# GpSimd's instructions chained in program order, with a job's transfers spaced eight chunks apart

## The chip, the cores and the metric

The kernel runs on one core of a Trainium2 chip. The metric is the device time of one execution in microseconds. Before the change three runs took 2229.27, 2233.75 and 2235.53 us, so the median is 2233.75. The profile was taken of a further execution of 2231.67 us.

## The reference

A trunk of two pre-norm residual layers over 256 tokens of width 2048, all in float32. Layer 0 mixes tokens with two-dimensional neighbourhood attention (16 heads of 128, a 4 x 64 grid, a window of 16 columns), layer 1 with a gated short convolution. After each mixer comes a gated MLP of inner width 5632 with a centred convolution of width 3 before the gate. A final RMSNorm closes it.

```python
def conv_glu_ffn(x, w_up, conv_w, conv_b, w_down):
    h = dwconv_centered(x @ w_up, conv_w) + conv_b
    g, u = jnp.split(h, 2, axis=-1)
    return (jax.nn.silu(g) * u) @ w_down

for i in range(DEPTH):                      # i = 0: attention, i = 1: short conv
    a = rms_norm(h, mix_norm[i])
    h = h + mixer(a)
    h = h + conv_glu_ffn(rms_norm(h, ffn_norm[i]), ...)
return rms_norm(h, final_norm)
```

The work is in the weight matrices: q, k, v and output of the attention, input and output of the convolution mixer, and two pairs of up- and down-projections.

## The kernel before

**Precision.** Every float32 operand is split into a high and a low part in the fast matmul format: ScalarE casts the high part (L186 for weights, L294 for activations), VectorE subtracts to get the low part (L189, L295). A product of two tiles is then three matmuls (high x high, high x low, low x high). In the projections with feature rows on the partitions (`Phase`: q and k, both up-projections, the convolution's input) the two parts of the activation lie side by side, so the first pass is one matmul of 512 columns (L255) and the second, with the low weights, one of 256 (L263).

**Chunks and items.** All weights arrive as chunks of up to 512 KB, in one list. `prep_to` goes along that list: it loads a chunk on SP's queue into one of six `raw` buffers and splits it. Matmul work is a list of items. The main loop takes them in order; for each it prepares its chunks, issues its matmuls, then prepares some chunks ahead (six after an up-projection item, four elsewhere) and calls `tick`, which runs delayed work that has come due. An up-projection item has two feature tiles, 64 matmuls and four chunks; there are 22 in a half of the MLP, or 27 with a few single ones at its start.

**Units with seven products.** In the output projections (`Tokens`) two blocks of 128 inner rows and two halves of the columns make a 2 x 2 block product. Written plainly, a pair costs eight products; the plans at L53 to L58 mark some pairs with H, and these take seven (`seven`, L460), with sums of blocks as operands. A plan holds the order of the pairs, the set of H, and the delay in ticks of `combine` (L486), which adds the unit's four extra accumulators into the residual stream. A unit needs two things made beforehand:

- sums of activations (`make_forms`, L513): four subtractions and additions on GpSimd (L519 to L522) into a tile `s`, as soon as the second of two neighbouring activation tiles is there. Four ticks later (`LATE`) ScalarE and VectorE split them (`splits`, into tiles `sf` and others). This happens during the up-projection, for the down-projection behind it; in an MLP half at every second item where the pair is marked.
- sums of weights, a *job* (`make`, L194): three transfers copy blocks of the weights to a piece of DRAM (`kept`), then two transfers on GpSimd's queue add another block to the first and second copy (L204, L205), then a third adds the first sum to the third copy (L208). The unit later loads the sums from there in place of weights (`kept` chunks in `prep_to`).

**Where jobs lie.** A job is an entry in the chunk list that loads nothing. `Phase` spreads its jobs over the items `hosts[0]` to `hosts[1]`, `Values` puts one after every second pair of chunks. The jobs' adding transfers are delayed by a number of chunks from the job: `ADDS, STORES = 2, 5` (L75). A group of jobs runs one phase or more ahead of the units that use it.

**Who orders the instructions.** Each engine runs its instructions in one fixed order, and a framework's scheduler sets that order from the program order and from what is ready. `load` (L160) forces weight loads on SP's queue into program order. The job's copies go through `load` too: each is queued behind the last weight load, but doesn't become the one that later loads are queued behind (`strict=False`). GpSimd's instructions have no such rule: the four form operations, the additions of mask and bias (L600), and the adding transfers stand as the scheduler puts them. A transfer issued by GpSimd waits on GpSimd for what it reads and writes, and what stands behind it waits too.

**The end.** The last down-projection keeps the last two pairs for `finale` (L445), which finishes one block of the output after the other, while the final norm of the blocks already done is computed.

Of the kernel before, what the change touches and what calls it, by code (L numbers as in the profile page):

```python
# [18 lines left out]
ALU = mybir.AluOpType  # L19
# [6 lines left out]
KT = D // P  # L26
NH = 16
GRID_W = 64
# [17 lines left out]
def plan(text, due):  # L46


    words = text.split()
    return (tuple(int(x[1:]) for x in words), {int(x[1:]) for x in words if x[0] == "H"}, due)  # L50


S_FIRST = (plan("P0 H1 H3 P2 H4 H5 P8 H6 H7 H9 P10", 3), plan("P0 P2 H1 H3 P8 H4 H5 H6 P10 H7 H9", 6))  # L53
S_SECOND = plan("P0 P2 H1 H3 H4 P9 H5 H6 H7 H8 P10", 0)
S_MLP = {(0, 0): S_FIRST, (0, 1): (S_SECOND, plan("P0 P2 P5 H1 H3 H4 P9 H6 H7 H8 P10", 0)),
         (1, 0): S_FIRST, (1, 1): (plan("P0 P2 H1 H3 H4 P9 H6 H7 H8 P5 P10", 1), plan("P0 P2 H1 H3 P5 H4 H6 H7 P8 P9 P10", 0))}
S_OUT = (plan("P0 H1 H2 P3 H4 H5 P6 P7", 1), plan("P0 P3 H1 H2 P6 H4 H5 P7", 0))
S_ATT = (plan("P0 P1 P2 H6 P3 H7 P4 P5", 1),) * 2  # L58
QK_JOBS, V_JOBS, UP_JOBS, SC_JOBS = (0, 2, 2, 0), (2, 2, 2, 0), (11, 10, 8, 10), 15


HEAD = (2, 4)
# [9 lines left out]
C_END = C_ID + P  # L72

LEAD = 96
ADDS, STORES = 2, 5  # L75
LATE = 4
RAWS = 6

# [2 lines left out]
def trunk(ctx, tc, xT, par, bias, wqk, wv, wo, wsc, wscout, wup, wdown, out):  # L81
    nc = tc.nc
# [44 lines left out]
    prepped = []  # L127

    stores = []
# [30 lines left out]
    def load(out, in_, strict=True):  # L160

        with ExitStack() as order:
            if "SP" in newest:
                order.enter_context(tc.issue_after(newest["SP"].ins))
            last = nc.sync.dma_start(out=out, in_=in_)
        if strict:
            newest["SP"] = last
# [24 lines left out]
    kept, newest, fenced = {}, {}, []  # L192

    def make(w, g, i):  # L194

        kept[id(w), g, i] = dst = dp.tile([P, 3, 4 * P], F32, name=f"kept{len(kept)}")
        l, r, t = (w[8 * g + f:8 * g + f + 4, :, (2 * i + k) * P:(2 * i + k + 1) * P].rearrange("f p c -> p f c")
                   for f, k in ((0, 0), (4, 0), (4, 1)))
        at = [dst[:, n].rearrange("p (f c) -> p f c", f=4) for n in range(3)]
        for n, x in ((0, l), (1, t), (2, t)):  # L200
            load(at[n], x, False)

        def adds():
            nc.gpsimd.dma_start(out=at[0], in_=r, accum_op=ALU.add)  # L204
            nc.gpsimd.dma_start(out=at[1], in_=r, accum_op=ALU.add)  # L205

        def store():
            nc.gpsimd.dma_start(out=at[2], in_=at[0], accum_op=ALU.add)  # L208
        stores.append((len(prepped) + ADDS, adds))
        stores.append((len(prepped) + STORES, store))  # L210

    jobs = []

    def plan_jobs(w, plans):
        jobs.extend((w, g, i) for g, (order, sset, _) in enumerate(plans) for i in order if i in sset)

    def take(n):
        out, jobs[:] = jobs[:n], jobs[n:]
        return out
# [54 lines left out]
    def after(n, fn):  # L274
        later.append((at[0] + n, fn))

    item = [0]
    at = [0]
# [9 lines left out]
    def split_into(hi, lo, src):  # L288

        with ExitStack() as order:  # L290
            if fenced:
                for x in ("ACT", "DVE"):
                    order.enter_context(tc.issue_after(newest[x].ins))
            first = nc.scalar.copy(out=hi, in_=src)  # L294
            nc.vector.tensor_sub(out=lo, in0=src, in1=hi.bitcast(F32))  # L295
        return first

    def split(dst, src):
        return split_into(dst[:, :S], dst[:, S:], src)
# [202 lines left out]
    def form_slots(blocks):  # L502

        if not form_at:
            return [left_over.pop() for _ in range(3)]
        tag = next(x for x in form_at if blocks == 3 or x != "sf")
        form_at.remove(tag)
        y = tp.tile([P, (6 if tag == "sf" else 8) * P], F32R, name="sf", tag=tag)
        if tag != "sf" and blocks == 3:
            left_over.append(y[:, 6 * P:])  # L510
        return y

    def make_forms(xe, xo, place, fresh=False):  # L513

        if fresh:
            form_at[:], left_over[:] = ("sf", "vv", "qk") * 2, ()
        v = tp.tile([P, 4, P], F32, name="s", tag="s")
        x11, x21, x12, x22 = (x[:, t * P:(t + 1) * P] for x in (xe, xo) for t in range(2))
        nc.gpsimd.tensor_sub(out=v[:, 0, :], in0=x21, in1=x22)  # L519
        nc.gpsimd.tensor_sub(out=v[:, 1, :], in0=v[:, 0, :], in1=x11)  # L520
        nc.gpsimd.tensor_add(out=v[:, 3, :], in0=x12, in1=v[:, 1, :])
        nc.gpsimd.tensor_sub(out=v[:, 2, :], in0=x11, in1=x21)  # L522
# [51 lines left out]
    a2 = [None] * KT  # L574
# [6 lines left out]
    def qk_evac(f, ps):  # L581
        c = both(ps, "g" if waiting and len(held) % 2 else "corr")
        if waiting:
            held.append(lambda: qk_rest(f, c))
        else:
            qk_rest(f, c)

    def qk_rest(f, c):
        h, which = divmod(f, 2)
        x = heads[h]  # L590
        t = tp.tile([P, S], F32, name="qk", tag="conv", bufs=4)
        nc.vector.tensor_mul(out=t, in0=c, in1=rstd)
        if which == 0:
            x["qk"] = tp.tile([P, 4 * S], F32R, name="qk", tag="qk")
        x["qk"[which]] = x["qk"][:, which * 2 * S:(which + 1) * 2 * S]
        first = split(x["qk"[which]], t)
        if which == 0:
            b = tp.tile([P, 6 * GRID_W], F32, name="bias", tag="sf")
            nc.sync.dma_start(out=b, in_=bias[:, h, :])
            nc.gpsimd.tensor_add(out=b.rearrange("p (i c) -> p i c", c=GRID_W),  # L600
                                 in0=b.rearrange("p (i c) -> p i c", c=GRID_W),
                                 in1=mask.unsqueeze(1).broadcast_to([P, 6, GRID_W]))
            x["b"] = b
        else:
            after((FIRST_HEADS[h] if h < len(FIRST_HEADS) else HEAD)[0], lambda: scores(h))
        return first
# [234 lines left out]
    def mlp(layer, a, evac):  # L841
        for half in range(2):
            act, forms = [None] * HALF, {}
            lo = half * HALF
            Phase(wup[layer], [f for j in range(lo, lo + HALF) for f in (2 * j, 2 * j + 1)], KT, a,
                  up_evac(layer, act, forms, S_MLP[layer, half]), intro=0 if half else 3,
                  jobs=take(UP_JOBS[2 * layer + half]), hosts=(3, 16) if half else (8, 22))
            Tokens(down[layer, half], HALF, act, evac if half else residual, S_MLP[layer, half], forms,
                   halves=4 if half and layer else 0)

# [2 lines left out]
    for half in range(2):  # L853
        plan_jobs(down[0, half], S_MLP[0, half])
    plan_jobs(wscout, S_OUT)
    for half in range(2):
        plan_jobs(down[1, half], S_MLP[1, half])
    for g in range(NH // 4):
        Phase(wqk, range(8 * g, 8 * g + 8), KT, a0, qk_evac, intro=0 if g else INTRO, step=STEP,
              jobs=take(QK_JOBS[g]), hosts=(0, 4))  # L860
        Values(g, a0, take(V_JOBS[g]))
    Tokens(wo, KT, oT, to_norm(1, a1), S_ATT, oforms)
    mlp(0, a1, to_norm(2, a2))
    Phase(wsc, range(3 * KT), KT, a2, sc_evac, intro=3, jobs=take(SC_JOBS), hosts=(8, 29))
    Tokens(wscout, KT, yT, to_norm(3, a3), S_OUT, yforms)
    mlp(1, a3, last_evac())


# [47 lines left out]
    for item[0], (ph, ft, c, k0, ka, kb) in enumerate(items):  # L916

        with ExitStack() as order:
# [4 lines left out]
            if item[0] != KT // STEP * INTRO:  # L923
# [3 lines left out]
                end, n = ends[item[0]], FURTHER if getattr(ph, "fence", False) else AHEAD  # L927
# [77 lines left out]
```

## Time and profile before

| | |
|---|---|
| runs, median (lowest to highest) | 2233.75 us (2229.27 to 2235.53) |
| profiled execution | 2231.67 us, span 2229.9 us |
| granted TensorE clock, mean | 0.992 |
| busy: PE, VectorE, ScalarE, GpSimd | 98%, 78%, 58%, 14% |
| jobs and units with seven products | 64 |

On the page each instruction group stands with its source line, so L189 is the low-part split of weights and L263 the low-part pass of a projection. PE busy is the time with a matmul under way. `kept<-in_wdown` is a job's copy if SP issued it, and an adding transfer if GpSimd (POOL) did; `kept<-kept` is the third adding transfer. A wait is put down to what came last. The chain of waits goes back from an instruction to what released it.

### The profile page before, as it was taken

To read this page: it belongs to the slowest core of one execution; us is meant where nothing else is said; L and a number is where in the kernel's file an instruction comes from. 1 tells how busy PE (TensorE), PEld (TensorE's weight loads), DVE (VectorE), ACT (ScalarE), POOL (GpSimd) and SP (SyncE) were. 2 spreads that over 40 slices of the span, in tenths; PEclk is the share of its full clock that TensorE was granted. 3 is DMA by queue.
4 is the path that set the end of the run, shared out by engine and by line. 5 is a ranking of instruction groups with operands and counts; after the bars stand their busy time and mean duration, and the time that the engine had idled before them with its cause. 6 is when DMAs were issued, how large, how long until landed. Compare 5 with 4: busy or idle time off the path is not lost.

```text
span 2229.9 us, 33099 instructions
## 1 busy us (share of the span) xinstructions
PE 2193.6 (98%) x11716; PEld 1900.0 (85%) x11716; DVE 1737.6 (78%) x2650; ACT 1286.3 (58%) x1985; POOL 308.2 (14%) x347
## 2 busy tenths in 40 slices
PE   9999999999899999999999999999999999999998
PEld 8788888888788888888888888888888888888886
DVE  8677667876688877788995676888768898778887
ACT  7555556654566655566664454666656666556565
POOL 1222010122200022200002222002220001221000
PEclk9999999999999999999999999999999999999999
DMA  9999557899868899967789999869996788998685
GB/s 285 273 280 253 183 167 229 239 270 250 233 212 269 264 278 256 267 206 228 251 269 279 270 297 268 282 221 266 278 226 203 243 274 278 262 279 236 200 263 170
DMA packets 411222, 555.32 MB, mean 249 GB/s; under 512 B 21680, under 2 KB 314672, under 8 KB 411056
## 3 DMA queue, kind: packets, MB, share of 16 engines
q1 hardware_dynamic: 332880, 502.23, 68.6%
q0 software_dynamic: 76800, 50.34, 17.1%
q8 instruction: 92, 1.51, 0.3%
q10 hardware_dynamic: 1376, 0.63, 0.1%
q14 instruction: 74, 0.61, 0.1%
HBM read 551.03 MB, written 102.76 MB: 293 GB/s over the span
## 4 chain that ended last, share of the span: by engine, by line
PE 79%; DMA 10%; DVE 5%; ACT 3%; issue 2%; POOL 1%; SPq 0%; DVEq 0%; ACTq 0%; POOLq 0%
PE mm L255 30%; PE mm L263 16%; DMA kept<-in_wdown 9%; PE mm L456 6%; PE mm L458 6%; PE mm L457 6%; PE mu L456 3%; PE mu L458 3%; PE mu L457 3%; DVE lo L189 2%; ACT hi L186 1%; PE mm L686 1%; PE mm L688 1%; PE mm L687 1%; PE tr L364 1%
## 5 line engine op out<-in xcount | busy, mean ns | idle before, releaser
L189 DVE TENSOR_TENSOR lo<-raw,hi 128x1024 fp32r<-128x1024 f32 (+1 forms) x856 | 1016.3, 1212 | 133.4 <-ACT hi L186 66.9
L186 ACT CAST hi<-raw 128x1024 fp32r<-128x1024 f32 (+1 forms) x920 | 914.5, 1010 | 347.1 <-PE mm L458 120.0
L255 PE MATMUL mm<-a,hi 128*128 128x512 f32 x4096 | 966.0, 392 | 0.4 <-DVE a L303 0.3
L255 PEld LDWEIGHTS mm<-a,hi 128*128 128x128 f32 x4096 | 762.9, 189 | 154.2 <-DVE a L303 1.2
L263 PEld LDWEIGHTS mm<-a,lo 128*128 128x128 f32 x4096 | 518.9, 193 | 34.9 <-DVE lo L189 22.5
L263 PE MATMUL mm<-a,lo 128*128 128x256 f32 x4096 | 526.7, 285 | 20.9 <-DVE lo L189 20.9
L332 ACT ACTIVATE conv<-pad,pt 128x256 f32<-128x256 f32 x176 | 105.6, 601 | 269.1 <-DVE pad L324 268.9
L456 PE MATMUL mm<-hi,act 128*128 128x512 f32 x634 | 247.5, 390 | 0.4 <-DVE corr L319 0.3
L458 PE MATMUL mm<-hi,act 128*128 128x512 f32 x634 | 246.7, 389 | 0.0
L457 PE MATMUL mm<-lo,act 128*128 128x512 f32 x576 | 224.4, 390 | 0.0
L334 DVE SCALAR_TENSOR_TENSOR conv<-pad,pt,conv 128x256 f32<-128x256 f32 x384 | 185.1, 484 | 34.9 <-ACT conv L332 25.9
L204 POOL DMA_DIRECT2D kept<-in_wdown x52 | 67.5, 1297 | 672.3 <-DMA kept<-in_wdown 671.9
L456 PEld LDWEIGHTS mm<-hi,act 128*128 128x128 f32 x634 | 119.0, 188 | 25.5 <-DVE corr L319 1.3
L458 PEld LDWEIGHTS mm<-hi,act 128*128 128x128 f32 x634 | 119.0, 188 | 24.8
L457 PEld LDWEIGHTS mm<-lo,act 128*128 128x128 f32 x576 | 108.2, 188 | 21.8
L319 DVE TENSOR_TENSOR corr<-mm,corr 128x256 f32<-128x256 f32 x256 | 106.2, 416 | 20.2 <-ACT corr L318 20.2
L318 ACT COPY corr<-mm 128x256 f32<-128x256 f32 x256 | 85.9, 368 | 60.2 <-PE mm L263 59.8
L208 POOL DMA_DIRECT2D kept<-kept x64 | 54.8, 855 | 400.9 <-DMA kept<-in_wdown 292.5
L295 DVE TENSOR_TENSOR sf<-s,sf 128x384 fp32r<-128x384 f32 (+2 forms) x37 | 19.1, 522 | 114.0 <-ACT sf L294 113.9
L295 DVE TENSOR_TENSOR act<-conv,act 128x256 fp32r<-128x256 f32 x88 | 37.6, 428 | 88.6 <-ACT act L294 88.6
L205 POOL DMA_DIRECT2D kept<-in_wdown x52 | 82.2, 1580 | 8.0 <-DMA kept<-in_wdown 7.0
L294 ACT CAST sf<-s 128x384 fp32r<-128x384 f32 (+2 forms) x37 | 17.2, 466 | 111.6 <-POOL s L520 102.7
(164 smaller groups left out, 1752.4 us busy)
## 6 DMA issues: line engine op xcount, KB each, us to landing
raw<-in_wup SPq DMA_DIRECT2D x352, 512.0 KB, 5.9
raw<-in_wdown SPq DMA_DIRECT2D x124, 512.0 KB, 4.8
raw<-in_wsc SPq DMA_DIRECT2D x96, 512.0 KB, 7.2
kept<-in_wdown SPq DMA_DIRECT2D x156, 256.0 KB, 8.6
raw<-kept SPq DMA_DIRECT2D x64, 512.0 KB, 5.0
raw<-in_wqk SPq DMA_DIRECT2D x56, 512.0 KB, 5.9
kept<-in_wdown POOLq DMA_DIRECT2D x104, 256.0 KB, 10.0
raw<-in_wv SPq DMA_DIRECT2D x32, 512.0 KB, 5.4
```

The costliest lines, as they stand in the source:

```text
L186: newest["ACT"] = nc.scalar.copy(out=hv, in_=r)
L189: newest["DVE"] = nc.vector.tensor_sub(out=lv, in0=r, in1=hv.bitcast(F32))
L205: nc.gpsimd.dma_start(out=at[1], in_=r, accum_op=ALU.add)
L255: nc.tensor.matmul(self.ps[ft], lhsT=prepped[i][0][:, o:o + P], rhs=self.src[k], start=k == 0, stop=False)
L263: nc.tensor.matmul(self.ps[ft][:, S:], lhsT=prepped[i][1][:, o:o + P], rhs=self.src[k][:, :S], start=False, stop=k == self.nk - 1)
L318: nc.scalar.copy(out=corr, in_=ps[:, S:])
L319: nc.vector.tensor_add(out=corr, in0=ps[:, :S], in1=corr)
L332: nc.scalar.activation(c, x[:, 1:S + 1], AF.Identity, scale=w[1], bias=b)
L334: nc.vector.scalar_tensor_tensor(out=c, in0=x[:, tap:tap + S], scalar=w[tap], in1=c, op0=ALU.mult, op1=ALU.add)
L456: nc.tensor.matmul(ps, lhsT=xh, rhs=wh, start=start, stop=False)
L457: nc.tensor.matmul(ps, lhsT=xh, rhs=wl, start=False, stop=False)
L458: nc.tensor.matmul(ps, lhsT=xl, rhs=wh, start=False, stop=stop)
```

## The change

Three things change together.

1. A new helper `pool` queues each instruction that it is given behind the previous one that it was given, on GpSimd: the four form operations, the bias addition, the adding transfers. GpSimd's order is then the program's.
2. The three copies of a job are issued by GpSimd, through the same helper, in place of SP. The first two adding transfers come eight chunks behind the job (`ADDS = 8`) in place of two, the third sixteen chunks behind it in place of five.
3. There are 67 units in place of 64: one more in the second half of layer 0's MLP and two more in that of layer 1's, where the plans of the two column groups are rewritten. The jobs are dealt out anew, and the items that host them begin earlier and end later: items 1 to 20 in place of 3 to 16 in second halves, 4 to 25 in place of 8 to 22 in first halves, 4 to 27 in place of 8 to 29 in the convolution's input.

```diff
-S_MLP = {(0, 0): S_FIRST, (0, 1): (S_SECOND, plan("P0 P2 P5 H1 H3 H4 P9 H6 H7 H8 P10", 0)),
-         (1, 0): S_FIRST, (1, 1): (plan("P0 P2 H1 H3 H4 P9 H6 H7 H8 P5 P10", 1), plan("P0 P2 H1 H3 P5 H4 H6 H7 P8 P9 P10", 0))}
+S_MLP = {(0, 0): S_FIRST, (0, 1): (S_SECOND, S_SECOND),
+         (1, 0): S_FIRST, (1, 1): (plan("P0 P2 H1 H3 H4 P9 H5 H6 H7 H8 P10", 0), plan("P0 P2 H1 H3 H4 P5 H6 H7 H8 P9 P10", 0))}
...
-QK_JOBS, V_JOBS, UP_JOBS, SC_JOBS = (0, 2, 2, 0), (2, 2, 2, 0), (11, 10, 8, 10), 15
+QK_JOBS, V_JOBS, UP_JOBS, SC_JOBS = (0, 2, 2, 0), (2, 2, 2, 0), (11, 11, 10, 11), 14
...
-ADDS, STORES = 2, 5
+ADDS = 8
...
         for n, x in ((0, l), (1, t), (2, t)):
-            load(at[n], x, False)
-
-        def adds():
-            nc.gpsimd.dma_start(out=at[0], in_=r, accum_op=ALU.add)
-            nc.gpsimd.dma_start(out=at[1], in_=r, accum_op=ALU.add)
-
-        def store():
-            nc.gpsimd.dma_start(out=at[2], in_=at[0], accum_op=ALU.add)
-        stores.append((len(prepped) + ADDS, adds))
-        stores.append((len(prepped) + STORES, store))
+            pool(nc.gpsimd.dma_start, out=at[n], in_=x)
+
+        def first():
+            for n in range(2):
+                pool(nc.gpsimd.dma_start, out=at[n], in_=r, accum_op=ALU.add)
+
+        def second():
+            pool(nc.gpsimd.dma_start, out=at[2], in_=at[0], accum_op=ALU.add)
+        stores.append((len(prepped) + ADDS, first))
+        stores.append((len(prepped) + 2 * ADDS, second))
+
+    def pool(op, **of):
+
+        with ExitStack() as order:
+            if "POOL" in newest:
+                order.enter_context(tc.issue_after(newest["POOL"].ins))
+            newest["POOL"] = op(**of)
...
-        nc.gpsimd.tensor_sub(out=v[:, 0, :], in0=x21, in1=x22)
...
+        pool(nc.gpsimd.tensor_sub, out=v[:, 0, :], in0=x21, in1=x22)
...
-            nc.gpsimd.tensor_add(out=b.rearrange("p (i c) -> p i c", c=GRID_W),
+            pool(nc.gpsimd.tensor_add, out=b.rearrange("p (i c) -> p i c", c=GRID_W),
...
-                  jobs=take(UP_JOBS[2 * layer + half]), hosts=(3, 16) if half else (8, 22))
+                  jobs=take(UP_JOBS[2 * layer + half]), hosts=(1, 20) if half else (4, 25))
...
-    Phase(wsc, range(3 * KT), KT, a2, sc_evac, intro=3, jobs=take(SC_JOBS), hosts=(8, 29))
+    Phase(wsc, range(3 * KT), KT, a2, sc_evac, intro=3, jobs=take(SC_JOBS), hosts=(4, 27))
```

The other three form operations are wrapped in the same way.

More of the change, by code (lines that the diff above doesn't have):

```diff
@@ L518, in make_forms @@
         x11, x21, x12, x22 = (x[:, t * P:(t + 1) * P] for x in (xe, xo) for t in range(2))
-        nc.gpsimd.tensor_sub(out=v[:, 0, :], in0=x21, in1=x22)
-        nc.gpsimd.tensor_sub(out=v[:, 1, :], in0=v[:, 0, :], in1=x11)
-        nc.gpsimd.tensor_add(out=v[:, 3, :], in0=x12, in1=v[:, 1, :])
-        nc.gpsimd.tensor_sub(out=v[:, 2, :], in0=x11, in1=x21)
+        pool(nc.gpsimd.tensor_sub, out=v[:, 0, :], in0=x21, in1=x22)
+        pool(nc.gpsimd.tensor_sub, out=v[:, 1, :], in0=v[:, 0, :], in1=x11)
+        pool(nc.gpsimd.tensor_add, out=v[:, 3, :], in0=x12, in1=v[:, 1, :])
+        pool(nc.gpsimd.tensor_sub, out=v[:, 2, :], in0=x11, in1=x21)
         if isinstance(place, tuple):
```

## The prediction

> **What bounds the kernel now.** I read the head of the page first, then the waits by engine.
>
> ```profile
> span 2229.9 us, 33099 instructions
> PE 2193.6 (98%) x11716; PEld 1900.0 (85%) x11716; DVE 1737.6 (78%) x2650; ACT 1286.3 (58%) x1985; POOL 308.2 (14%) x347
> POOL kept L204 <- DMA kept<-in_wdown: 671.9, 38, 143.1
> POOL kept L208 <- DMA kept<-in_wdown: 292.5, 48, 8.7
> ACT sf L294 <- POOL s L520: 102.7, 24, 11.2
> SPq L165 <- DVE lo L189: 1324.8, 699, 16.5
> PE mm L263 <- DVE lo L189: 20.9, 8, 5.2
> PE tr L639 <- DVE act L295: 4.5, 1, 4.5
> ```
>
> (Columns of the waits: total us, times, longest.) The matmul engine is busy 98% of the span, so a change pays by removing matmuls or by removing the few waits of PE. One group of waits is large: eight times the second half of an up-projection item (the low-part matmuls of L263) waits for VectorE's split L189, 20.9 us together. VectorE is not full (78%), so I followed the chain of waits back from the longest of the eight.
>
> ```profile
> 578.42 8.68 DMA kept<-in_wdown
> 587.38 0.87 POOL kept L208
> 589.29 0.52 ACT sf L294
> 589.84 0.35 DVE sf L295
> 590.60 1.14 DVE lo L189
> 591.79 3.79 PE mm L263 x16
> ```
>
> GpSimd issued a first adding transfer at 578.42, then stood 8.68 us until it had landed, because the second one (L208) is next in its order. The form of the activations (L519 to L522) sat behind that wait. ScalarE's and VectorE's splits of the form stood in their own orders, and the weight splits that PE needed stood behind them. GpSimd's and SP's timelines just before show a whole job, and what the copies have to do with it:
>
> ```profile
> 564.24 1.28 POOL L204 DMA_DIRECT2D kept<-in_wdown  x1 [2.33 <-DMA kept<-in_wdown]
> 578.42 1.28 POOL L204 DMA_DIRECT2D kept<-in_wdown  x1 [2.87 <-DMA kept<-in_wdown]
> 563.90 4.73 SPq L165 DMA_DIRECT2D raw<-in_wup  x4
> 568.69 3.21 SPq L165 DMA_DIRECT2D kept<-in_wdown  x3
> ```
>
> The copies (three per job, last row) stand in SP's order behind weight loads that wait for free buffers (1324.8 us in all), and GpSimd waits for them at L204 (2.33 and 2.87 us here), and then for its own first transfer at L208.
>
> **What the eight waits cost.** A clean item lasts 11.11 us (491.53 to 502.64). PE's timeline gives the four disturbed stretches, each from the start of a hit item to the next start at the old pace:
>
> ```profile
> 491.53 7.44 PE L255 MATMUL mm<-a,hi 128*128 128x512 f32 x32
> 498.81 4.00 PE L263 MATMUL mm<-a,lo 128*128 128x256 f32 x32
> 502.64 7.44 PE L255 MATMUL mm<-a,hi 128*128 128x512 f32 x32
> 607.55 7.44 PE L255 MATMUL mm<-a,hi 128*128 128x512 f32 x32
> 873.29 7.44 PE L255 MATMUL mm<-a,hi 128*128 128x512 f32 x32
> 952.27 7.44 PE L255 MATMUL mm<-a,hi 128*128 128x512 f32 x32
> 1356.22 7.44 PE L255 MATMUL mm<-a,hi 128*128 128x512 f32 x32
> 1368.60 7.44 PE L255 MATMUL mm<-a,hi 128*128 128x512 f32 x32
> 1954.65 7.44 PE L255 MATMUL mm<-a,hi 128*128 128x512 f32 x32
> 1969.85 7.44 PE L255 MATMUL mm<-a,hi 128*128 128x512 f32 x32
> ```
>
> The first holds eight items: 607.55 - 502.64 - 8 x 11.11 = 16.0. The second holds six: 952.27 - 873.29 - 6 x 11.11 = 12.3. The last two hold one each: 1.3 and 4.1. Sum 33.7 us: the 20.9 idle and 12.8 more, because PE runs at a lower clock after a long wait:
>
> ```profile
> 595.37 8.51 PE L255 MATMUL mm<-a,hi 128*128 128x512 f32 x32
> 484.00:606.00 122.00, 111.71 (x614) 97.85 (x613) 84.65 (x142) 60.36 (x101) 32.51 (x38) 0.96 0.97 252
> ```
>
> The item after the 5.24 us wait takes 8.51 where 7.44 is usual. (The stretch row has PE, PEld, DVE, ACT, POOL busy, then granted clock, DMA share, GB/s: clock 0.96 over this first stretch.)
>
> **The change, part by part.** *Order and spacing on GpSimd.* The first adding transfers now stand eight chunks behind the copies, the second eight further. An up-projection item has four chunks, and a phase with hosts (1, 20) places 11 jobs over 19 items, 0.58 per item. Eight chunks are then 8 / 4.58 = 1.75 items, 19.4 us. The landing times of these transfers stay below that:
>
> ```profile
> DMA to landing us min/median/max: 2.8/7.2/14.8
> L204 POOL DMA_DIRECT2D kept<-in_wdown x52: 1267/1277/1615, 120.0 to 2013.2; - x52
> L205 POOL DMA_DIRECT2D kept<-in_wdown x52 | 82.2, 1580 | 8.0 <-DMA kept<-in_wdown 7.0 <-issue 0.9
> L208 POOL DMA_DIRECT2D kept<-kept x64 | 54.8, 855 | 400.9 <-DMA kept<-in_wdown 292.5 <-DMA kept<-in_wscout 52.7 <-DMA kept<-in_wo 24.7
> ```
>
> So a wait is over, or nearly, when GpSimd reaches it. GpSimd may run ahead of program time and meet a transfer too early, but it can only run ahead to its next form, so such a wait falls into the gap before that form. The gap: forms come every second item, 22.2 us apart; 1.16 jobs in it are 3.5 copies, 2.3 first and 1.2 second transfers, 3.5 x 1.3 + 2.3 x 1.45 + 1.2 x 0.86 = 9 us of issue, or some 18 us with one whole landing of about 9 us (8.68 above) in between. That fits. The form itself is then ready about 2.3 us after its inputs; its splits are placed four ticks, one item, later. I take all eight waits as gone: **-33.7 us**. Bounds: -33.7, and 0 if the waits only move (their cover is the gap above; without it each late form costs what the eight cost now, 4.2 us on average).
>
> *The copies leave SP for GpSimd.* SP loses 192 issues and gains no time from it, for it waits on buffers anyway. GpSimd gains 3 x 67 issues. A plain copy of this shape is not in the trace on GpSimd; the nearest rows are L204 and L205, 1.3 to 1.6 us, so 261 to 318 us, and the three more jobs' adds 11: GpSimd goes from 308 to some 580 to 640 us, under 30%. All of it lies in the gaps: 0 us, with the bound of the third rival if it doesn't.
>
> The Trainium skill speaks against this part twice. "DMA: Bandwidth & Descriptors", section "SWDGE vs HWDGE vs iDMA", gives plain transfers to SP or ACT and only adding ones to GpSimd, whose descriptors are computed by software; its first byte is about 0.4 us later by the page's latency figures, an estimate of 80 us over 201 copies, none of it on the path when nobody waits. "SBUF — State Buffer", section "Who interferes with whom", says that VectorE's two-port operations keep GpSimd from writing descriptors. Here the issue took 1267, 1277 and 1615 ns at the least, the median and the most, so nothing of the kind shows; the page agrees that two-input operations, which fill VectorE here, don't take that port.
>
> *Three more units with seven products.* Each drops one product of three matmuls. The 32 wide matmuls of an item take 498.81 - 491.53 = 7.28 us, 0.2275 each: 9 x 0.2275 = **-2.0 us**. VectorE pays:
>
> ```profile
> L189 DVE TENSOR_TENSOR lo<-raw,hi 128x1024 fp32r<-128x1024 f32 (+1 forms) x856 | 1016.3, 1212 | 133.4 <-ACT hi L186 66.9 <-PE mm L263 54.6 <-issue 5.6
> L151 DVE TENSOR_TENSOR raw<-raw 128x512 f32<-128x512 f32 x64 | 44.2, 691 | 1.8
> 2140.00:2160.00 20.00, 20.00 (x90) 16.57 (x89) 19.88 (x25) 13.78 (x18) 0.00 (x0) 1.00 0.93 312
> 2209.24 0.69 DVE L353 TENSOR_TENSOR h<-mm,h 128x512 f32<-128x512 f32 x1 [1.04 <-PE mm L458]
> 2206.30:2219.30 13.00, 13.00 (x63) 9.98 (x61) 8.57 (x26) 6.29 (x17) 0.00 (x0) 1.00 0.11 32
> ```
>
> A pair with eight products needs two splits, 2.4 us; a unit three of 1.21, a half one and an add of 0.69, 5.0 us, against 21 x 0.2275 = 4.8 us of PE. A group of seven units and four pairs asks 35 + 9.7 + 8.2 (four residual and eight combining operations of 0.68) = 53 us of VectorE against 55.3 of PE, so it stays hidden, as in the stretch 2140 to 2160 where VectorE is busy 19.88 of 20 and PE doesn't wait. One place has no cover: in the last group unit 8 now stands directly ahead of the closing part, and its combination (about 4.9 us of VectorE) falls between that part's start and its first residual, where VectorE idles 1.04 us today. The closing part (last row) lasts 13.0 us with VectorE idle for 4.4 of them, so nearly all can be absorbed: between 0 and +4.9, I take **+1.0**, nearer to the row with room.
>
> *Placement.* More even jobs (0.58 per item for 0.8) lower the DMA share from the 0.97 above. From the chunk list, the closest second transfer stands 49 chunks ahead of the load that reads it, some 85 us. Both 0.
>
> **Sum.** On the profiled execution, 2231.67 us with its span of 2229.9: -33.7 - 2.0 + 1.0 = -34.7, so 2197.0. The median of the runs shown, 2233.75, is 2.1 above; from there 2199.1. I say **2198**.
>
> **Rivals.** *Part of the waits stays:* GpSimd meets landings that take longer, because six transfers share its one queue instead of three. The row with 14.8 us against 19.4 speaks against it; that half of the waits needs only one slow landing in each phase speaks for it. Half of 33.7 gives 2215.
>
> *The early wait goes too:* PE's 4.5 us at L639, with about 2 of slow clock behind it, comes from loads of the value weights in a stretch with copies; they may come sooner without copies ahead of them in SP's order. 2198 - 6.5 = 2191.
>
> *Slower: GpSimd's queue falls behind.* A job every 19.1 us with six transfers leaves 3.2 us for each; from there it decides. At 3.8 us a job is 22.8, the backlog grows 3.7 us per job, 41 us in a phase of 11; less the 9 us of slack of a form (one item less 2.3), 32 us of forms late in each of five phases: 2197 + 160, about 2357. For it: the first of two adding transfers issued together took 8.68 us to land, over 4 each if they share alike. Against it: a job took 564.24 to 578.42, 14.2 us, with all its six transfers and a full weight stream.
>
> *The change doesn't do what it says:* the splits are late for another reason, and new waits eat the gain, say 2231. The chain above names GpSimd plainly, so little is left for it.
>
> **How the numbers follow.** Forecast 0.60, part 0.18, early wait too 0.07, no effect 0.07, slower 0.08. What a measurement tells from no change is 0.3%, 6.7 us: faster below 2227. Faster 0.60 + 0.18 + 0.07 = 0.85, same 0.07, slower 0.08. The range takes the first three with their bounds: 2189 (early wait gone, closing part free) to 2222 (a third of the gain), leaving 0.15 outside.
>
> **What would show it.** PE's waits on L189 at L263 gone or under 5 us, granted clock 1.00 in the up-projection stretches; GpSimd's waits on transfers far below 671.9 and 292.5, or lying ahead of other transfers and not of forms; ScalarE's wait for L520 well under 102.7; GpSimd busy 580 to 640 us. In the closing part, the first residual should come later than today against the last unit. I am wrong if PE waits on L263 in numbers like today's, if weight loads get late (ScalarE waiting for raw tiles before its split), or if PE waits in the last 25 us for more than 4 us.

## The result, and the profile after

The changed kernel takes 2211.01 us (median of 4 runs, 2208.13 to 2212.37) against 2233.17 for the kernel before in the same comparison: a ratio of 0.9901, 95% interval 0.9883 to 0.9918. It is faster by 22 us, inside the predicted range; the forecast of 2198 asked for 35. One experiment below, with paced copies, had two of its ten executions at 2346.9 and 3639.3 us, at granted clocks of 0.87 and 0.56; they are left out of its ratio, their cause stays open, and no other kernel here had one.

The head of the changed kernel's page, and then its waits by engine (total us, times, longest). L262 and L270 are what L255 and L263 were before, L463 to L465 the former L456 to L458, and every instruction that goes through the helper has line L217.

```profile
span 2208.4 us, 33010 instructions
PE 2184.2 (99%) x11707; PEld 1890.4 (86%) x11707; DVE 1744.9 (79%) x2664; ACT 1307.3 (59%) x1996; POOL 468.3 (21%) x561
```

```profile
PE mm L463 <- DVE h L360: 7.4, 3, 5.4
POOL s L217 <- DVE conv L752: 952.1, 28, 165.4
POOL kept L217 <- DMA kept<-in_wdown: 180.8, 37, 8.6
ACT sf L301 <- POOL s L217: 34.5, 32, 1.2
```

No wait of PE for a weight split in an up-projection is left. GpSimd now waits for the inputs of its forms (952.1) far longer than for transfers (180.8, where before 671.9 and 292.5 stood at the two adding lines), and ScalarE waits 34.5 us for forms where it was 102.7. But a new wait of PE heads the list, in the output projections.

PE's timeline splits the execution into stages, each from the start of its first matmul to the start of the next stage's. Lengths in us, one profiled execution of each kernel; the kernels of the last four columns are explained below. The stages left out differ by 0.4 us at most between before and after:

| stage | before | after | chain alone | spacing alone | short spacing | paced copies |
|---|---|---|---|---|---|---|
| first values | 30.28 | 23.99 | 23.99 | 31.62 | 23.99 | 23.99 |
| attention's output projection | 89.12 | 96.39 | 89.12 | 89.12 | 89.26 | 89.13 |
| layer 0, first up | 262.93 | 246.90 | 246.92 | 260.97 | 246.92 | 246.89 |
| layer 0, first down | 110.19 | 110.19 | 110.19 | 110.70 | 110.19 | 110.19 |
| layer 0, second up | 256.76 | 244.46 | 244.47 | 256.61 | 244.47 | 244.47 |
| layer 0, second down | 112.63 | 125.98 | 112.63 | 112.63 | 120.85 | 111.95 |
| convolution's input | 270.36 | 269.12 | 269.11 | 272.78 | 269.12 | 269.55 |
| layer 1, first down | 111.18 | 110.19 | 110.19 | 112.24 | 110.19 | 110.19 |
| layer 1, second up | 248.56 | 244.46 | 244.46 | 246.42 | 244.47 | 244.46 |
| layer 1, second down and end | 126.69 | 125.70 | 127.82 | 127.48 | 127.08 | 126.13 |

From before to after the up-projections and the convolution's input give 16.03 + 12.30 + 1.24 + 4.10 = 33.7 us, the first values 6.3, the two down-projections of layer 1 1.0 each: 42.0. Two output projections take back 7.27 + 13.35 = 20.6. That leaves 21.4 of the 21.5 by which the spans differ.

The two stages that got longer, before and then after (window; length, then PE, PEld, DVE, ACT, POOL busy, granted clock, DMA share, GB/s):

```profile
311.06:400.18 89.12, 89.12 (x413) 74.31 (x412) 67.36 (x81) 51.78 (x72) 4.83 (x8) 1.00 0.63 201
1030.06:1142.69 112.63, 112.63 (x507) 93.49 (x506) 100.70 (x120) 75.05 (x93) 0.00 (x0) 1.00 0.82 264
```

```profile
304.58:400.97 96.39, 91.02 (x413) 75.47 (x412) 67.59 (x81) 51.96 (x72) 17.12 (x21) 0.96 0.75 221
1002.52:1128.50 125.98, 118.26 (x504) 93.87 (x503) 103.17 (x123) 76.01 (x95) 19.70 (x20) 0.97 0.97 289
```

PE did its work there without a gap before; now it idles 5.4 and 7.7 us and runs at a clock of 0.96 and 0.97. What is new in these stages is GpSimd, busy 17 and 20 us. Its timeline after, at the start of the two (start, us, count):

```profile
320.57 4.50 POOL L217 DMA_DIRECT2D kept<-in_wdown  x6
325.31 7.39 POOL L217 DMA_DIRECT2D kept<-in_wdown  x7 [0.25 <-issue]
...
994.39 4.79 POOL L217 DMA_DIRECT2D kept<-in_wscout  x6
1002.59 8.22 POOL L217 DMA_DIRECT2D kept<-in_wscout  x8 [3.42 <-DMA kept<-in_wscout]
```

These transfers belong to jobs that the program places in the phase behind, from 400.97 and 1128.50 on. They depend on nothing but DRAM and each other, and no form stands ahead of them in an output projection. GpSimd issues thirteen in 12 us: nine copies and four adding transfers (the paced version below, with a mark ahead of each job's three copies, has three marks among the same thirteen). Only then comes the phase's first form, and GpSimd waits for its input:

```profile
453.87 0.46 POOL L217 TENSOR_TENSOR s<-conv 128x128 f32<-128x128 f32 x1 [121.17 <-DVE conv L752]
```

The weight loads of that moment suffer. DMA issues after, from 304 to 350 us (count, KB each, median us from issue to landing), and the row of the same stretch before:

```profile
raw<-in_wo SPq DMA_DIRECT2D x13, 512.0 KB, 12.2
kept<-in_wdown POOLq DMA_DIRECT2D x13, 256.0 KB, 10.1
```

```profile
raw<-in_wo SPq DMA_DIRECT2D x13, 512.0 KB, 4.9
```

The landing goes from 4.9 to 12.2 us, and ScalarE stands for it; the waits in that stage after:

```profile
ACT hi L186 <- DMA raw<-in_wo: 13.7, 7, 3.7
PE mm L463 <- DVE h L360: 5.4, 1, 5.4
```

### The profile page after: what moved, and what is told of

Same layout as the page of the kernel before. It is cut to its first block, busy times and chain, and to the rows that moved or that the text cites. A ratio compares the mean times of both kernels' runs of the same rounds, so it can differ in the third digit from the quotient of the medians.

```text
span 2208.4 us, 33010 instructions
## 1 busy us (share of the span) xinstructions
PE 2184.2 (99%) x11707; PEld 1890.4 (86%) x11707; DVE 1744.9 (79%) x2664; ACT 1307.3 (59%) x1996; POOL 468.3 (21%) x561
## 4 chain that ended last, share of the span: by engine, by line
PE 94%; DMA 2%; DVE 2%; ACT 1%; issue 1%; DVEq 0%; ACTq 0%
PE mm L262 42%; PE mm L270 22%; PE mm L463 6%; PE mm L464 6%; PE mm L465 6%; PE mu L463 2%; PE mu L465 2%; PE mu L464 2%; PE mm L693 1%; PE mm L694 1%; PE mm L695 1%; DVE lo L189 1%; DMA raw<-in_wo 1%; DMA raw<-in_wdown 1%; PE tr L371 1%
## 5 line engine op out<-in xcount | busy, mean ns | idle before, releaser
L262 PE MATMUL mm<-a,hi 128*128 128x512 f32 x4096 | 961.8, 391 | 0.5 <-DVE a L310 0.3
L262 PEld LDWEIGHTS mm<-a,hi 128*128 128x128 f32 x4096 | 759.7, 188 | 152.9 <-DVE a L310 1.2
L270 PEld LDWEIGHTS mm<-a,lo 128*128 128x128 f32 x4096 | 512.9, 192 | 11.8
L270 PE MATMUL mm<-a,lo 128*128 128x256 f32 x4096 | 518.1, 283 | 0.0
L217 POOL DMA_DIRECT2D kept<-in_wdown x275 | 276.5, 1672 | 88.8 <-DMA kept<-in_wdown 82.2
L463 PE MATMUL mm<-hi,act 128*128 128x512 f32 x620 | 243.4, 393 | 8.1 <-DVE h L360 7.4
L465 PE MATMUL mm<-hi,act 128*128 128x512 f32 x620 | 242.1, 391 | 0.0
L217 POOL TENSOR_TENSOR s<-conv 128x128 f32<-128x128 f32 x56 | 26.3, 470 | 952.1 <-DVE conv L752 952.1
L325 ACT COPY corr<-mm 128x256 f32<-128x256 f32 x256 | 93.1, 369 | 135.8 <-PE mm L270 135.1
L463 PEld LDWEIGHTS mm<-hi,act 128*128 128x128 f32 x620 | 117.0, 189 | 34.1 <-issue 6.9
L465 PEld LDWEIGHTS mm<-hi,act 128*128 128x128 f32 x620 | 117.0, 189 | 24.3
L217 POOL DMA_DIRECT2D kept<-kept x67 | 70.6, 1072 | 126.6 <-DMA kept<-in_wdown 98.6
L463 PE MATMUL mu<-hi,sf 128*128 128x512 f32 x189 | 74.5, 394 | 1.9 <-ACT hi L186 1.9
L464 PE MATMUL mu<-lo,sf 128*128 128x512 f32 x189 | 74.6, 395 | 1.2 <-DVE lo L189 1.2
```

What stands on the lines that cost most here:

```text
L217: newest["POOL"] = op(**of)
L262: nc.tensor.matmul(self.ps[ft], lhsT=prepped[i][0][:, o:o + P], rhs=self.src[k], start=k == 0, stop=False)
L270: nc.tensor.matmul(self.ps[ft][:, S:], lhsT=prepped[i][1][:, o:o + P], rhs=self.src[k][:, :S], start=False, stop=k == self.nk - 1)
L325: nc.scalar.copy(out=corr, in_=ps[:, S:])
L463: nc.tensor.matmul(ps, lhsT=xh, rhs=wh, start=start, stop=False)
L464: nc.tensor.matmul(ps, lhsT=xh, rhs=wl, start=False, stop=False)
```

## The experiments

Two questions: which part of the change took the eight waits away (the prediction prices order and spacing as one part and argues from the spacing), and whether the 20.6 us are lost because GpSimd runs ahead, or because its copies are bad for the weight loads wherever they lie.

**The chain alone.** The kernel before, with every GpSimd instruction through `pool` and nothing else: copies on SP, spacing 2 and 5, 64 units, old placement.

```diff
-            nc.gpsimd.dma_start(out=at[0], in_=r, accum_op=ALU.add)
+            pool(nc.gpsimd.dma_start, out=at[0], in_=r, accum_op=ALU.add)
...
-        nc.gpsimd.tensor_sub(out=v[:, 0, :], in0=x21, in1=x22)
+        pool(nc.gpsimd.tensor_sub, out=v[:, 0, :], in0=x21, in1=x22)
```

> The kernel before with one part of the change: GpSimd's forms, bias additions and adding transfers are chained in program order; copies on SP, spacing 2 and 5 chunks, 64 units, as before. If the spacing is what removed the eight waits (my theory), the waits stay: the first up-projection of layer 0 near 263 us, its second near 257, about 2230 us in all. If the order was what mattered, these fall to 247 and 245 and the whole to about 2200 us.

> The kernel before with GpSimd's instructions chained in program order and nothing else, taken again for an interval. The theory that the order alone removes the eight waits and the early one (33.7 + 6.3 us, and 1.2 to 1.8 in the stages sc and the first down-projection of the second layer) says 2231.7 - 41 = 2191, within 3. If the first look was an accident of one execution, it comes back between 2200 and 2230.

The first run gave 2192.31, the repeat 2190.58 (2189.23 to 2192.41), ratio 0.9819, interval 0.9801 to 0.9836. All eight waits in the up-projections are gone, and the early one (the repeat is the column "chain alone"). The wide spacing is not needed for it. PE's longest wait in the whole repeat is this:

```profile
PE bc L810 <- DVE conv L808: 1.6, 1, 1.6
```

**The spacing alone.** The kernel before with one line changed.

```diff
-ADDS, STORES = 2, 5
+ADDS, STORES = 8, 16
```

> The kernel before with only the spacing changed: the adding transfers come 8 and 16 chunks behind the job in place of 2 and 5; no chain, copies on SP, 64 units and the old placement. If the spacing is what removed the eight waits: the up-projections fall by 16.0, 12.3, 1.3 and 4.1 us, and no output projection is slower, about 2232 - 33.7 = 2198 us; the early wait on the value weights (about 6.3 us in the stage of the first values) stays if it comes from copies ahead of weight loads on SP, else about 2192. If the free order puts transfers ahead of forms again, some of the waits stay: 2205 to 2225 us.

Measured 2235.24, with 2233.57 for the kernel before. The eight waits and the early one are all there:

```profile
PE mm L263 <- DVE lo L189: 21.3, 8, 4.0
PE tr L639 <- DVE act L295: 4.7, 1, 4.7
```

Why a distance of eight chunks in the program has no effect shows in the order in which GpSimd's instructions run. In the kernel before and in this one, all 64 third transfers stand directly behind the second one of the same job, whatever the program wrote between them, and a form often stands directly behind the third. GpSimd's timeline in the run with the spacing alone (L519 is the first operation of a form), and then with the chain alone:

```profile
549.77 1.28 POOL L204 DMA_DIRECT2D kept<-in_wdown  x1 [3.17 <-DMA kept<-in_wdown]
550.54 1.78 POOL L205 DMA_DIRECT2D kept<-in_wdown  x1
560.61 0.85 POOL L208 DMA_DIRECT2D kept<-kept  x1 [8.29 <-DMA kept<-in_wdown]
561.18 0.77 POOL L519 TENSOR_TENSOR s<-conv 128x128 f32<-128x128 f32 x1
```

```profile
541.52 2.85 POOL L217 DMA_DIRECT2D kept<-in_wdown  x2
561.70 0.46 POOL L217 TENSOR_TENSOR s<-conv 128x128 f32<-128x128 f32 x1 [17.33 <-DVE conv L752]
...
563.68 0.85 POOL L217 DMA_DIRECT2D kept<-kept  x1
```

In the first, L208 waits out the landing of its own first transfer, and the form waits with it. With the chain, 23 of the 64 third transfers have a form or a bias addition ahead of them, and the landing passes behind it. Counted over the whole trace, form operations begin at 37 places in the kernel before: 36 of them lie directly behind a third transfer, and at 31 the form starts as soon as that one is issued. With the chain alone they begin at 30 places, and at every one GpSimd sits idle first, waiting for the form's input. The spacing is only a wish until something holds the order.

**Only the transfers chained**, the forms and bias additions left free.

> The kernel before with only the adding transfers chained to each other in program order; the forms and the bias additions on GpSimd stay free to be put anywhere. If what matters is the place of the forms among the transfers, the waits stay: 2225 to 2235. If it is the order of the transfers among themselves, they go: about 2191.

One run gave 2219.54: between the two theories, with five of the eight waits and part of the early one left. All 64 third transfers again stand directly behind their second ones, and at 30 of 37 places a form starts as soon as a third transfer is issued. So most of the gain hangs on the place of the forms among the transfers; what took the other three waits away was not followed.

```profile
PE mm L270 <- DVE lo L189: 15.5, 5, 4.8
PE tr L646 <- DVE act L302: 3.0, 1, 3.0
```

**The early wait.** It goes with the chain, also where copies stay on SP. Two views of the kernel before: the DMA issues between 40 and 64 us (count, KB each, median us to landing) for the value weights, and GpSimd's timeline at its first adding transfers.

```profile
raw<-in_wv SPq DMA_DIRECT2D x6, 512.0 KB, 8.7
```

```profile
45.12 1.42 POOL L204 DMA_DIRECT2D kept<-in_wo  x1 [11.36 <-DMA kept<-in_wo]
```

The same two views with the chain alone (the repeat):

```profile
raw<-in_wv SPq DMA_DIRECT2D x6, 512.0 KB, 6.3
```

```profile
61.59 2.69 POOL L217 DMA_DIRECT2D kept<-in_wo  x2
```

The chain puts the first transfers behind bias additions, 16 us later, and the value weights land sooner. That fits, and in the run with only the transfers chained they stayed early; but the two were not tried apart.

**Parts added to the chain with copies on SP.** First the units: plans and numbers of jobs for 67 on the chain alone. Second the spacing of 8 and 16 on the chain alone. Third the changed kernel with its copies on SP, which has both, and the new placement:

```diff
-            pool(nc.gpsimd.dma_start, out=at[n], in_=x)
+            load(at[n], x, False)
```

> Chain in program order and 67 units; copies on SP, spacing 2 and 5, and placement as before. The theory that the units cost and pay what the prediction said (-2.0 for nine matmuls, +1.0 in the closing part) gives 1.0 us less than the chain alone: about 2191. A rival, that VectorE's extra work or the three more jobs bring new waits, gives the chain alone plus 2 to 6, about 2194 to 2198.

> Chain in program order, and adding transfers eight and sixteen chunks behind the copies; copies on SP, 64 units and placement as before. The theory that the order does it all says the spacing adds nothing: the chain alone within 2 us, about 2190 to 2194. The rival, that the spacing is what costs the version with copies on SP its 4 us against the chain alone, gives about 2196 to 2198.

> The changed kernel with one part undone: the three copies of a job are issued by SP again, as before; GpSimd's chain, the spacing of eight chunks and the 67 units stay. Theory A (GpSimd, with nothing to wait for behind its last form, issues the next phase's copies at once, and this burst starves the weight loads of the two output projections that lost time): with the copies paced by SP's order of weight loads the burst is gone. The output projection of the attention falls from 96.4 us back to 89.1 or less, the second one of layer 0's MLP from 126.0 to about 110.2; the up-projections stay at 246.9 and 244.5. About 2211 - 7.3 - 15.8 = 2188 us if the early wait on the value weights stays away, 2194 if it comes back with copies ahead of weight loads on SP. Theory B (the load comes from the units: 67 in place of 64, with adding transfers spaced so that they run during the projections): both stages keep their loss, 2205 to 2211 us.

Units: 2194.85 (2192.54 to 2199.47), ratio 0.9844 (0.9822 to 0.9866). Spacing: 2200.71 (2197.71 to 2203.36), 0.9863 (0.9844 to 0.9882). Both with the placement: 2196.74 (2194.48 to 2199.21), 0.9835 (0.9813 to 0.9858). None beats the chain alone, and the spacing's interval lies clear of its own; the other two overlap with it. The profiles show waits of PE for VectorE in the output projections, longer than the 0.3 and 1.4 us in the two runs of the chain alone. The one of the units' run, and then that of the spacing's:

```profile
PE mm L463 <- DVE corr L326: 2.7, 1, 2.7
```

```profile
PE mm L463 <- DVE corr L326: 5.3, 4, 2.4
```

Why the wide spacing costs some 10 us on this chain is open. The profiled executions differ by 6.3 us, and three output projections hold it: layer 0's second down-projection (114.63 for 112.63), the convolution's (85.88 for 83.62) and the last stage (129.9 for 127.8). With copies back on SP the burst is gone: the attention's output projection lasts 89.11 us and layer 0's second down-projection 114.05. The time is still above the 2188 expected for it; 3.6 us of that lie in layer 1's first up-projection (250.38 for 246.81), which was not followed.

**Copies on GpSimd with the short spacing.** First on the chain alone (old placement, 64 units), then the changed kernel with only the spacing undone (new placement, 67 units), whose edit is this:

```diff
-ADDS = 8
+ADDS, STORES = 2, 5
...
-        stores.append((len(prepped) + 2 * ADDS, second))
+        stores.append((len(prepped) + STORES, second))
```

> Chain in program order, and the copies issued by GpSimd; spacing 2 and 5, 64 units, placement as before. Two theories of the 20 us that the changed kernel loses in the output projections. One: it is a burst. GpSimd runs ahead into the jobs of the next phase because nothing stands between their copies; with adding transfers two chunks behind the copies it meets its own landings and paces itself. Then little is lost, 0 to 8 us against the chain alone: 2192 to 2200, and the output projection of the attention lasts under 92 us. Two: copies issued by GpSimd hurt the weight loads by themselves, however they are spaced: then 15 to 20 us are lost, 2207 to 2212, and that stage lasts 95 us or more.

> The changed kernel with the adding transfers two and five chunks behind the copies again; chain, copies on GpSimd, 67 units and placement stay. The theory that copies on GpSimd need the wide spacing, because GpSimd otherwise waits for its own copies ahead of the forms, expects waits of PE on VectorE's weight split in the up-projections as in the version with 64 units: 2235 to 2250, the output projection of the attention near 89 us. If the even placement alone already takes these waits away, 2195 to 2215.

The first takes 2245.12 (2239.76 to 2249.45), ratio 1.006 (1.0041 to 1.008): slower than before. Neither theory had foreseen that. Its attention's output projection is clean (89.12), which speaks for the burst, but the waits of the up-projections are back:

```profile
PE mm L270 <- DVE lo L189: 33.0, 7, 6.5
```

The second takes 2201.03 in one run, and its up-projections are clean. They differ in the placement and three units, which were not tried apart, and the timelines point to why that is worth 44 us. GpSimd's timeline between two forms (each form is four TENSOR_TENSOR rows; the first is shown), old placement:

```profile
499.36 2.29 POOL L217 DMA_DIRECT2D kept<-in_wdown  x3
503.01 1.27 POOL L217 DMA_DIRECT2D kept<-in_wdown  x1 [1.36 <-DMA kept<-in_wdown]
504.46 1.26 POOL L217 DMA_DIRECT2D kept<-in_wdown  x1 [0.18 <-issue]
513.99 0.85 POOL L217 DMA_DIRECT2D kept<-kept  x1 [8.27 <-DMA kept<-in_wdown]
514.54 2.60 POOL L217 DMA_DIRECT2D kept<-in_wdown  x3
523.80 2.56 POOL L217 DMA_DIRECT2D kept<-in_wdown  x2 [6.67 <-DMA kept<-in_wdown]
525.35 1.49 POOL L217 TENSOR_TENSOR s<-conv 128x128 f32<-128x128 f32 x1
```

The same view with the new placement and the short spacing, and then of the changed kernel itself:

```profile
492.84 2.29 POOL L217 DMA_DIRECT2D kept<-in_wdown  x3
496.57 2.56 POOL L217 DMA_DIRECT2D kept<-in_wdown  x2 [1.44 <-DMA kept<-in_wdown]
507.63 0.85 POOL L217 DMA_DIRECT2D kept<-kept  x1 [8.50 <-DMA kept<-in_wdown]
512.88 0.47 POOL L217 TENSOR_TENSOR s<-conv 128x128 f32<-128x128 f32 x1 [4.40 <-DVE conv L752]
```

```profile
500.49 0.86 POOL L217 DMA_DIRECT2D kept<-kept  x1
501.07 5.13 POOL L217 DMA_DIRECT2D kept<-in_wdown  x5
520.58 0.46 POOL L217 TENSOR_TENSOR s<-conv 128x128 f32<-128x128 f32 x1 [14.38 <-DVE conv L752]
```

A job with its own landings in GpSimd's order takes 15.6 us (492.84 to 508.48). Forms come every 22.2. The old placement puts parts of two jobs between two forms, 26 us from 499.36, and the form is late; the new one puts one job there, and 4.4 us of waiting for the input remain. The wide spacing lengthens that reserve to 14.4 us, and no stage of the up-projections gains from it. It costs something instead: the short spacing makes GpSimd wait for its own copies, so it cannot run far ahead, and the attention's output projection stays at 89.26. It doesn't cure the other stage, where 120.85 is still 8 us too long, and the convolution's output projection grows from 83.62 to 85.83.

**Moving the burst, and stopping it.** Later hosts in the first halves and the convolution's input:

```diff
-                  ... hosts=(1, 20) if half else (4, 25))
+                  ... hosts=(1, 20) if half else (11, 27))
...
-    Phase(wsc, ..., hosts=(4, 27))
+    Phase(wsc, ..., hosts=(13, 29))
```

> The changed kernel with another placement only: in the first halves of the MLPs the jobs lie on items 11 to 27 in place of 4 to 25, in the convolution's input on items 13 to 29 in place of 4 to 27, so that all copies of these phases stand behind the phase's first form in GpSimd's order. GpSimd still issues them. Theory A: GpSimd has to wait at the first form, so nothing is issued during the two output projections; they fall to 89.1 and about 110.2 us, the sum to about 2188 us. If copies on GpSimd's queue are what harms (Theory C: plain transfers on that queue take bandwidth from weight loads wherever they lie), the loss moves into the up-projections, where GpSimd's transfers now lie closer together: 2200 to 2211 us, with PE waits at the weight splits there.

2204.44 (2202.99 to 2206.31), ratio 0.9868 (0.985 to 0.9886). That fits neither theory: the two stages are clean (89.12 and 111.96) and no up-projection is longer, but layer 0's first down-projection and the convolution's output projection, 110.19 and 83.62 in the changed kernel, now hold the loss, with 3.1 us more in layer 1's first down-projection (113.28). GpSimd issues 18 transfers between 629 and 662 us, around the start of the first of them, where the changed kernel has 12 between 633 and 655. Layer 0's stage and the convolution's as windows (columns as above):

```profile
640.14:757.80 117.66, 112.84 (x489) 90.76 (x487) 97.49 (x110) 70.09 (x80) 8.72 (x10) 1.00 0.93 287
1383.32:1472.93 89.61, 87.05 (x379) 69.88 (x377) 74.30 (x92) 55.38 (x73) 4.25 (x4) 0.98 0.88 266
```

The last run keeps the changed kernel whole and takes away only the running ahead. ScalarE copies one column of the newest weight tile, and GpSimd reads it ahead of a job's copies:

```diff
+    marks = ep.tile([P, 72], F32, name="marks")
...
+        newest["hi"] = hi
...
+        m = len(kept) - 1
+        nc.scalar.copy(out=marks[:, m:m + 1], in_=newest["hi"][:, :1].bitcast(F32))
+        pool(nc.gpsimd.tensor_add, out=marks[:, 71:72], in0=marks[:, m:m + 1], in1=marks[:, m:m + 1])
         for n, x in ((0, l), (1, t), (2, t)):
             pool(nc.gpsimd.dma_start, out=at[n], in_=x)
```

> The changed kernel, with one thing added: ahead of each job's three copies ScalarE copies one column of the newest weight tile's high part, and GpSimd adds that column to itself, so that the copies can't start before the weight stream has reached the job's place. Copies on GpSimd, spacing of eight, 67 units and placement stay. If the 20.6 us are lost because GpSimd runs ahead into the next phase's jobs in a burst, the output projection of the attention comes back from 96.4 to about 89.1 us and the first layer's second down-projection from 126.0 to about 112.6; with some new lateness of a microsecond or two 2211 falls to 2188 to 2196. If copies from GpSimd hurt the loads wherever they lie, the same loss comes back at other places and it stays at 2205 to 2215.

> The changed kernel with its copies paced by the weight stream, taken again, because one of its four times (2346.9 against 2188.7 to 2189.6) left the interval open. If that one was a disturbance of the chip, the median comes back at 2189, within 3, and the ratio to the kernel before at 0.977 to 0.984. If the paced version has a second, slow way of running, times near 2347 come back.

2189.22 and, again, 2189.28, ratio 0.9816 (0.9801 to 0.983). Both stages are back; their windows, then GpSimd's longest wait, and the mark ahead of the copies that the changed kernel starts at 320.57:

```profile
303.55:392.68 89.13, 89.13 (x414) 74.33 (x413) 67.49 (x81) 51.91 (x74) 5.94 (x10) 1.00 0.63 201
994.23:1106.18 111.95, 111.95 (x504) 92.94 (x503) 102.04 (x122) 76.14 (x95) 0.00 (x1) 1.00 0.82 268
```

```profile
POOL marks L222 <- ACT marks L203: 648.6, 22, 130.3
```

```profile
392.03 0.19 POOL L222 TENSOR_TENSOR marks<-marks 128x1 f32<-128x1 f32 x1 [72.44 <-ACT marks L203]
```

GpSimd stands 648.6 us in front of copies that it used to issue at once, and the whole 20.6 us come back with copies on GpSimd, spacing and placement unchanged. So the loss is the burst. The chain alone, 1.3 us behind it in another comparison, needs none of the other parts, and it beats both the kernel before and the changed one.

## Why the prediction was right, and where not

**What bounds the kernel, and the eight waits: right.** They were worth 16.0 + 12.3 + 1.3 + 4.1 us by the prediction, and the stages give 16.03, 12.30, 1.24 and 4.10. The chain of waits through GpSimd's landing, the late form and the late split was the right one: the chain that moves the forms ahead of the landings takes the waits away, and the kernel that brings two jobs between two forms brings them back. One reading was off in size: 8.68 us is the landing, while GpSimd itself, which issued L205 first, stood 6.42 us of it before L208.

**"The first adding transfers now stand eight chunks behind": the wrong part of the change.** The step costed order and spacing as one and argued from 19.4 us against the longest landing of 14.8. The spacing alone changes nothing, since the written order is not kept; with copies on SP the chain with the old spacing does it all. The prediction had the evidence in the rows it quoted (a transfer landing from 578.42 on, and L208 at 587.38 waiting for it) and did not ask why a third transfer written three chunks later stood there.

**"... it can only run ahead to its next form, so such a wait falls into the gap before that form": the step that failed.** It holds in the up-projections, where forms stand at every second item. In the stages ahead of a phase the next form is far away: GpSimd issued thirteen transfers at once from 320.57 on and then stood for 121 us until the form's input came, at 453.87. Such bursts cost 20.6 us in two output projections, and the sum had nothing for them. The prediction named the sign of it among what would make it wrong (ScalarE waiting for raw tiles before its split), but put no price on it.

**Placement, put at 0: wrong in what it hides.** With copies on GpSimd and the short spacing the old placement takes 2245 and the new one, with three more units, 2201. Under the wide spacing it was not tried alone.

**The copies' cost: right that the issue is hidden, too high in size.** GpSimd is busy 468.3 us, not 580 to 640: less the 11 us forecast for the three more jobs' adding transfers, (468.3 - 308.2 - 11) / 201 is 0.74 us for a copy, where the adding rows of 1.3 to 1.6 had been taken for it. The advice that the prediction took from the Trainium skill, "DMA: Bandwidth & Descriptors", section "SWDGE vs HWDGE vs iDMA", to leave plain copies to SP, would have been worth 2211.01 - 2196.74 = 14.3 us here, more than the 0 of the sum. Its reason, slower set-up, is not what the runs show: with pacing, the version with copies on GpSimd takes 2189.3.

**The early wait** was given 0.07, and it went (-6.3). The rival's reason, SP rid of copies, is not needed, since the chain alone with copies on SP does the same. The two errors, +20.6 and -6.3, partly cancel; with the 1.0 of layer 1's first down-projection they make up the distance from 2198 to 2211.

**Units and closing part: right in sum, not to be told from nothing.** The second down-projection of layer 0 shows one unit's 0.68 us (112.63 to 111.95) in the paced version. The last stage changes by -0.99 where -1.36 + 1.0 was forecast, so the closing part costs 0.4, less than the 0.8 by which this stage differs between the two runs of the chain alone. On the chain alone the units gave no gain (2194.85 against 2190.58, intervals overlapping).

**The slower rival** (GpSimd's queue falls behind) did not come, but the run at 2245 comes near it, at another point: not the mean rate of transfers, but the number of jobs between two forms.

## What to carry to other kernels

Before pricing a distance between instructions, look at the order in which they stand on the engine: a scheduler that is free will undo a distance, and an order held by a chain can be worth more than any distance. Then ask for each instruction freed of its waits what stops it from running too early: work that waits for nothing is issued in a burst at the next quiet place, and the price is paid by whoever shares the transfers there. On an in-order engine, count how many self-made landings lie between two of its instructions that others wait for.

## What the runs showed of the hardware that was not expected

Nine copies and four adding transfers of 256 KB, issued by GpSimd in 12 us, raised the landing of 512 KB weight loads from 4.9 to 12.2 us, though the DMA share of the whole stage was only 0.75. The Trainium skill, "DMA: Bandwidth & Descriptors", section "Queues, rings and completion order", says that an engine takes turns between the queues that have work, packet by packet; by that alone two queues with equal packets would double a load's time, an estimate, and the trace shows 2.5 times. The landing counts from the issue, so queueing behind earlier loads is in it; the rest is not settled.

Six copies from DRAM to DRAM in a row took GpSimd 4.50 us to issue (320.57 above), 0.75 us each; two adding transfers of the same size in a row took 2.56 us (496.57 above).

After five of PE's eight waits in the kernel before, those of 2.07 to 5.24 us, the matmuls that followed ran at about half pace for a while: in the trace the wide ones start 427 ns apart after four of them, where 227 is usual, and the narrow ones 214 ns apart after the fifth (2.37 us, at 1966.37), where 120 is usual. After the three waits of 0.83 to 1.79 us the pace was the usual one. Beyond their idle time these five cost 10.7 of the 12.8 us that the prediction found.
